# A gated mLSTM and convolution block: operand-group loads placed behind weight pieces, posts with a deadline, and another split of the down projection

## The chip, the cores and the metric

The kernel runs on one core of a Trainium2 chip, as one launch. The metric is the device time of one execution in microseconds (us). Before and after are compared by the median of several executions.

## The reference, cut to what matters

One residual block on x of 512 tokens by 2048 channels, all in float32. An RMS norm and one wide projection (w_in) give queries, keys, values, gates and convolution inputs; an mLSTM over 4 heads and a short causal convolution are each projected to 2048 channels (w_branch_m, w_branch_c), merged by sigmoid gates, projected by w_out and added to x. Then comes the channel mixer, which the down part of the change is about:

```python
hn = rmsnorm(h, norm_ffn_g)
u = causal_dwconv(hn @ w_up, ffn_conv_w, ffn_conv_b)      # 2048 -> 2 x 5504
gate, val = jnp.split(u, 2, axis=-1)
h = h + (jax.nn.silu(gate) * val) @ w_down                # 5504 -> 2048
return rmsnorm(h, norm_out_g)
```

## The kernel before, in words

**Products.** Every float32 operand is split into a high part, which ScalarE writes (a copy to the fp32r type), and a low part, which VectorE writes (the operand minus its high part). A product is three matmuls: high with high, high with low, low with high. Most of the work goes through a scheme with seven products in place of eight for a 2 x 2 block of tiles, so sums of weight tiles and of operand tiles have to be made first. Some pieces use all eight products and need no sums of weights; they are the last piece of each item in w_bc, w_bm, w_out and the down projection.

**Steps.** An item is a pair of output tiles. It takes `nq` steps; a step works off one weight piece (4 k tiles by 2 output tiles) against two operand groups, with 42 matmuls (48 with eight products). The first two and the last two items of a phase take turns, step by step. The phases, with the numbers of their steps: w_in 0 to 159, w_bc 160 to 175, w_bm 176 to 191, w_out 192 to 223, up 224 to 395, down 396 to 475, and 16 steps at the end (476 to 491) for the last three k tiles. The down projection is done in parts, given by `CHUNKS` (L37) as first k tile and number of pieces; each part adds its result to `h_d` in memory with an accumulating DMA from the POOL queue (L155).

**What a step issues** (loop from L291). In step s the low parts of piece s + 1 (L235, L189) and of the groups planned for s + 1 (L359) are written, the sums of piece s + 2 (L216, L221) and of the groups planned for s + 2 (L342, L347, L352, or L337 for groups used with eight products) are made, and the high parts follow. So a group planned for step k has its sums in step k - 2 and its low part in step k - 1, as piece k has. VectorE runs all this in the order written. When an item ends, ScalarE copies one product out of the accumulator (L303) and four VectorE additions (L309 to L312) in the next step form the result z.

**Loads.** A piece that needs sums is loaded in two stages: SP's queue fetches two tiles (L250, L251), and when they have landed, POOL's queue adds two others to them with accumulating DMAs (L253); a further DMA of SP brings the four tiles as they are (L260). A group takes two DMAs of 256 KB (L326). Pieces and groups share a ring of six raw buffers (`RAW`, L33). They are loaded in one fixed order, `order` (L1084): before, a group planned for step k stands just ahead of piece k. `load_next` (L1089) issues the next load when fewer than six loads are without their low parts; it counts finished low parts in `n_lo`. `loads` (L1097) is called at the end of each step and issues all it can; `load_to` forces the loads that the step needs. Groups of the up projection are scaled by ScalarE ahead of their sums: five are read from memory, the last three come straight from the item's z by two scalings (L394), with a raw buffer and no DMA.

**Posts.** What follows an item's end (normalizing, gates, convolution, silu, store) is a list of parts with costs, in us of VectorE. The planner adds 5.04 to a credit each step and takes off the cost of all VectorE work issued: 0.8 for the sums and 2.05 for the low parts of a piece (0 and 1.5 with eight products), 1.35 and 1.95 for a group (0.65 and 1.7; 1.35 more for sums that take in a z), 2.3 for the four additions. An up item's post has five parts: 1.2, 0, 1.4, 1.4 and 0.7. A part with a cost is issued only if credit is above half of it, unless the post is urgent. What is left when a later item ends is run at once, by `flush` (L1126), ahead of that item's copy (L303). For the up and down items that later item is three further on.

The loop that issues posts (L1385 to L1393), and the plan of the groups' steps (L1070 to L1081):

```python
cost, fn = x[1][0]
if not rush and cost and credit <= cost / 2:
    break
...
k = max(k, all_cells[n - 8].last + 3, t.after, t.spread)
if tasks[k]:
    k += 1
t.k = k
cells_at.setdefault(k, []).append(t)
tasks[k].append(t)
```

Of the kernel before, what the change touches and what calls it, by code (L numbers as in the profile page):

```python
# [33 lines left out]
NC = NW // 2  # L34
ACTS = 8
ALONE = ((0, 0), (1, 0), (0, 1), (0, 2))
CHUNKS = [(0, 4), (16, 3), (28, 3)]  # L37
K_LAST = 40


# [4 lines left out]
def kpair(c):  # L45

    q, r = divmod(c, 2)
    return 4 * q + r, 4 * q + 2 + r


class Item:


    def __init__(self, load, nq, xs, post, pre=None, eight=None):
        self.load, self.nq, self.xs, self.post, self.pre, self.eight = load, nq, xs, post, pre, eight
        self.p1_start, self.urgent, self.done = True, False, False
        self.set = self.num = self.z = self.buf = None
        self.p1_end = 2 * nq - (3 if eight == nq - 1 else 1)


class Task:


    def __init__(self, load, sums, hi, lo, ready=None):
        self.load, self.sums, self.hi, self.lo, self.ready = load, sums, hi, lo, ready
        self.wh = self.wl = None
        self.raw, self.cost, self.plain, self.after_end, self.pre = None, (0.8, 2.05), False, None, None


@with_exitstack  # L70
def tile_block(ctx: ExitStack, tc: tile.TileContext, xT, w1, w_v0, w_v1, w_v2, w_bm, w_bc, w_out, w_up, w_down,
# [13 lines left out]
    def nm(s):  # L85
        uid[0] += 1
        return f"{s}_{uid[0]}"

    def f(ap):
        return ap.bitcast(F32)  # L90
# [4 lines left out]
    def slots(t):  # L95
        return t.rearrange("p (s n) -> p s n", n=SW)

    def two(ap):
        return ap.unsqueeze(1).to_broadcast([P, 2, ap.shape[-1]])
# [215 lines left out]
    def cell_task(xs, c, d, scale=None, key=None, eight=False):  # L315

        k1, k2 = kpair(c) if isinstance(c, int) else c
        t = Task(None, None, None, None)

        def new_raw():  # L320
            t.raw = wp.tile([P, NW], F32, tag="raw", name=nm("xraw"), bufs=RAW)

        def load():
            new_raw()
            for dst, k in zip(t.two(), (k1, k2)):
                SP.dma_start(dst, d[k])  # L326

        def two_k():
            return (t.raw[:, :T], t.raw[:, T:2 * T]) if eight else (t.raw[:, 5 * SW:], t.raw[:, :2 * SW])

        def scaled():
            for ap, k in zip(two_k(), (k1, k2)):
                A.activation(ap, ap, AF.Copy, scale=scale(k))

        def diff():
            x = slots(t.raw)
            V.tensor_sub(x[:, 4:6], x[:, 0:4:2], x[:, 1:4:2])  # L337

        def t3():
            x = slots(t.raw)  # L340

            V.tensor_sub(x[:, 2:4], x[:, 1:6:4], two(x[:, 6]))  # L342

        def e():

            x = slots(t.raw)
            V.scalar_tensor_tensor(x[:, 4], x[:, 3], -1.0, x[:, 1], op0=ALU.mult, op1=ALU.subtract)  # L347

        def t4():

            x = slots(t.raw)
            V.scalar_tensor_tensor(x[:, 6], x[:, 4], -1.0, x[:, 0], op0=ALU.mult, op1=ALU.subtract)  # L352

        def hi():
            t.act = actp.tile([P, 2 * NW], F32R, tag="act", name=nm("act"))
            A.activation(t.act[:, :m], t.raw[:, :m], AF.Copy)  # L356

        def lo():
            V.tensor_sub(t.act[:, NW:NW + m], t.raw[:, :m], f(t.act[:, :m]))  # L359
            t.raw = None  # L360
            xs[t.cell] = t.act
            t.act = None

        t.load, t.sums, t.hi, t.lo, t.new_raw = load, [diff] if eight else [t3, e, t4], hi, lo, new_raw
        t.two, m = two_k, 6 * SW if eight else NW
        t.pre = scaled if scale else None
        t.cost = (0.65, 1.7) if eight else (1.35, 1.95)
        t.ready = (lambda: all(k in stored for k in key)) if key else None
        return t

    def direct_cell(xs, c, it, d=None, scale=None, key=None, eight=False):

        t = cell_task(xs, c, d, None, key, eight)
        cell_t3, cell_load = t.sums[0], t.load
        k1, k2 = kpair(c)

        def load():
            if d is not None:
                cell_load()
            else:  # L380
                t.new_raw()

        def t3():
            assert it.done
            a, b = t.two()
            V.tensor_add(a, a, it.z[:, :T])
            V.scalar_tensor_tensor(b, it.z[:, T:], -1.0, b, op0=ALU.mult, op1=ALU.subtract)
            it.z_read = True
            cell_t3()

        def scaled():
            assert it.done
            for ap, z, k in zip(t.two(), (it.z[:, :T], it.z[:, T:]), (k1, k2)):
                A.activation(ap, z, AF.Copy, scale=scale(k))  # L394
            it.z_read = True

        it.z_read = False
        t.load = load
        if d is not None:
            t.sums = [t3] + t.sums[1:]  # L400
        else:
            t.pre = scaled
        t.cost = (t.cost[0] + (1.35 if d is not None else 0), t.cost[1])
        t.after_end = it
        return t
# [464 lines left out]
    steps, items_all, all_cells = [], [], []  # L870
# [119 lines left out]

    for c, (k0, nq) in enumerate(CHUNKS):
        AA = {}
# [43 lines left out]
    def last_act():  # L1036
        t = Task(None, None, None, None)
        m = NL * T

        def load():  # L1040
            t.raw = wp.tile([P, NW], F32, tag="raw", name=nm("xraw"), bufs=RAW)
            for i in range(NL):
                SP.dma_start(t.raw[:, i * T:(i + 1) * T], a_d[K_LAST + i])

        def hi():
            t.act = actp.tile([P, 2 * NW], F32R, tag="act", name=nm("act"))
            A.activation(t.act[:, :m], t.raw[:, :m], AF.Copy)

        def lo():
            V.tensor_sub(t.act[:, m:2 * m], t.raw[:, :m], f(t.act[:, :m]))  # L1050
            t.raw = None
            plain["x"] = t.act
            t.act = None

        t.load, t.sums, t.hi, t.lo = load, [], hi, lo
        t.cost = (0, 1.7)
        t.ready = lambda: all(("a", K_LAST + i) in stored for i in range(NL))
        return t

    e_last = len(steps)  # L1060
    t = last_act()
    t.cell, t.first, t.last, t.after, t.spread, t.xs = "x", e_last, e_last + 15, 0, e_last - 4, plain
    all_cells.append(t)
    n_main = len(steps)
    steps.extend((l, 0) for l in lasts)


    tasks = [[] for _ in range(len(steps) + 1)]
    wt = [weight_task(it, q) if isinstance(it, Item) else last_weight(it.n) for it, q in steps]
    k, cells_at = 0, {}  # L1070
    for n, t in enumerate(all_cells):
        if n < 8:
            k = t.cell
        else:
            k = max(k, all_cells[n - 8].last + 3, t.after, t.spread)
            if tasks[k]:
                k += 1
            t.k = k
            cells_at.setdefault(k, []).append(t)
            assert k <= t.first, (n, k, t.first)  # L1080
        tasks[k].append(t)  # L1081
    for s, t in enumerate(wt):
        tasks[s].append(t)
    order = [t for ts in tasks for t in ts]  # L1084
    place = {id(t): i for i, t in enumerate(order)}
    at = [place[id(t)] for t in wt] + [len(order) - 1] * 8
    n_load, n_lo, held = [0], [0], [0]

    def load_next():  # L1089
        i = n_load[0]  # L1090
        if i == len(order) or i - n_lo[0] + held[0] == RAW or (order[i].ready and not order[i].ready()):
            return False
        order[i].load()
        n_load[0] += 1
        return True

    def loads():  # L1097
        while load_next():
            pass
# [5 lines left out]
    def lo_ops(t):  # L1105

        def done():
            n_lo[0] += 1

        if isinstance(t.wh, list):  # L1110
            return [lambda: t.lo(0), lambda: (t.lo(1), done())]
        return [lambda: (t.lo(), done())]
# [123 lines left out]
    for i in range(at[START]):  # L1236
# [4 lines left out]
        while todo_mm:  # L1241
            s, r = todo_mm[0]
            it, q = steps[s]
# [41 lines left out]
    credit = 0.0  # L1285
    urgent = {it.num for it in items_all if it.urgent}


    finals, lq, lsum = deque(), [], []

    for s in range(START, len(steps)):
        it, q = steps[s]
# [89 lines left out]
        if s >= START + hold:  # L1382
            credit = min(credit, 2.5)
            rush = not main or any(x[0] in urgent for x in posts)
            for x in list(posts)[:2]:  # L1385
                cost, fn = x[1][0]
                if not rush and cost and credit <= cost / 2:
                    break
                x[1].popleft()
                credit -= cost  # L1390
                fn()
                if not x[1]:
                    posts.remove(x)  # L1393
        for t in cells_at.get(s + 3, []):
            if t.pre and t.raw is not None and (not t.after_end or t.after_end.done):
                t.pre()
                t.pre = None
# [10 lines left out]
        if not main and it.n > 11 and finals:  # L1408
            for _ in range(2):
                if finals:  # L1410
                    last_scale(0, finals.popleft(), row0)
        loads()
    for l in lq:
        last_post(l)
    for l in lsum + lq:
# [68 lines left out]
```

## Time and profile before

| | us |
|---|---|
| median of 3 runs | 2645.81 (2645.74 to 2651.76) |
| the profiled execution, its own time | 2654.39 |
| its span, first to last instruction | 2652.7 |

The profile is of one execution of its own. Its span is 1.7 us shorter than that execution's time. TensorE is PE for matmuls and PEld for weight loads, VectorE is DVE, ScalarE is ACT, GpSimd is POOL, SyncE is SP. L and a number is a line of the kernel before. "<-" and a name stand for what ended an idle time.

### The profile page before, as it was taken

Reading aid. Unit: us, or ns where it says so; the run is one execution under the profiler, and the core shown is the slowest. Engines: PE = TensorE matmul, PEld = TensorE weight load, DVE = VectorE, ACT = ScalarE, POOL = GpSimd, SP = SyncE. Lnnn points to the kernel's source line nnn. Section 1 sums busy time; section 2 is a strip of 40 time slices with the busy share of each in tenths; the row PEclk is TensorE's granted clock in tenths of the full one; section 3 lists DMA queues with packets and bytes.
Section 4 is the critical chain, followed back from the end, with each engine's and each line's share of the span. In section 5 each row is a group of like instructions: output and inputs, shape, how many; then the busy total and the mean of one; then the engine's idle time right before and its main releaser. Section 6 shows DMA issues by size and latency. Waiting matters only on the chain.

```text
span 2652.7 us, 55503 instructions
## 1 busy us (share of the span) xinstructions
PE 2584.3 (97%) x21146; PEld 2564.9 (97%) x21146; DVE 2112.7 (80%) x3308; ACT 1291.1 (49%) x1748; POOL 796.4 (30%) x922
## 2 busy tenths in 40 slices
PE   8999999999999999899999999999999989999998
PEld 8999999999999999899899999999999989999997
DVE  8577778886777888877989888888888887676756
ACT  6444554546556543345555445444444544444433
POOL 2443333333333111221333333333333223232320
PEclk8999999999999999999999999999999999999999
DMA  7798989998898797887998889989888888898976
GB/s 216 181 228 229 240 223 253 221 252 225 231 248 219 227 298 208 218 244 209 236 224 227 221 221 227 225 219 225 222 222 220 209 219 210 200 239 195 233 173 203
DMA packets 462557, 592.55 MB, mean 223 GB/s; under 512 B 42784, under 2 KB 296736, under 8 KB 462288
## 3 DMA queue, kind: packets, MB, share of 16 engines
q1 hardware_dynamic: 301968, 419.79, 50.4%
q0 software_dynamic: 133088, 124.04, 31.4%
q10 hardware_dynamic: 27232, 45.17, 4.7%
q8 instruction: 165, 2.70, 0.4%
q14 instruction: 104, 0.85, 0.1%
HBM read 531.17 MB, written 57.67 MB: 222 GB/s over the span
## 4 chain that ended last, share of the span: by engine, by line
PE 54%; DVE 6%; DMA 3%; issue 2%; ACT 0%; POOL 0%; DVEq 0%; SPq 0%; POOLq 0%; ACTq 0%
PE bank L281 18%; PE bank L279 18%; PE bank L280 17%; DMA raw<-in_w_down_dram 2%; DVE wl L235 1%; DVE act L359 1%; DMA raw<-in_w_out_dram 1%; DVE z L310 0%; PE bank L440 0%; PE bank L1164 0%; PE bank L1165 0%; PE bank L1166 0%; DMA raw<-in_w_up_dram 0%; DVE z L309 0%; DMA h_d<-z 0%
## 5 line engine op out<-in xcount | busy, mean ns | idle before, releaser
L281 PE MATMUL bank<-act,wl 128*128 128x256 f32 x6760 | 1922.7, 284 | 33.5 <-DVE wl L235 28.5
L279 PE MATMUL bank<-act,wh 128*128 128x256 f32 x6760 | 1931.1, 286 | 14.3 <-ACT z L303 5.8
L280 PE MATMUL bank<-act,wh 128*128 128x256 f32 x6760 | 1919.3, 284 | 0.0
L281 PEld LDWEIGHTS bank<-act,wl 128*128 128x128 f32 x6760 | 1303.9, 193 | 39.4 <-DVE wl L235 33.4
L279 PEld LDWEIGHTS bank<-act,wh 128*128 128x128 f32 x6760 | 1304.2, 193 | 18.8 <-ACT z L303 6.5
L231 ACT ACTIVATE wh<-raw 128x896 fp32r<-128x896 f32 x856 | 812.1, 952 | 1036.9 <-PE bank L280 679.5
L280 PEld LDWEIGHTS bank<-act,wh 128*128 128x128 f32 x6760 | 1304.3, 193 | 2.8 <-issue 1.7
L235 DVE TENSOR_TENSOR wl<-raw,wh 128x896 fp32r<-128x896 f32 x856 | 929.1, 1087 | 343.1 <-PE bank L281 231.7
L253 POOL DMA_DIRECT2D raw<-in_w_up_dram x344 | 298.5, 941 | 603.4 <-DMA raw<-in_w_up_dram 371.9
L253 POOL DMA_DIRECT2D raw<-in_w_dram x280 | 244.1, 961 | 527.1 <-DMA raw<-in_w_dram 344.9
L216 DVE TENSOR_TENSOR raw<-raw 128x256 f32<-128x256 f32 x428 | 179.6, 420 | 37.3 <-DMA raw<-in_w_down_dram 23.1
L253 POOL DMA_DIRECT2D raw<-in_w_down_dram x112 | 100.9, 1032 | 282.2 <-DMA raw<-in_w_down_dram 107.4
L221 DVE TENSOR_TENSOR raw<-raw 128x256 f32<-128x256 f32 x428 | 179.0, 418 | 0.3
L309 DVE TENSOR_TENSOR z<-bank,z 128x512 f32<-128x512 f32 x131 | 89.8, 686 | 38.4 <-ACT z L303 28.3
L356 ACT ACTIVATE act<-xraw 128x1792 fp32r<-128x1792 f32 (+1 forms) x52 | 85.6, 1646 | 60.2 <-DVE xraw L352 49.5
L184 ACT ACTIVATE wh<-raw 128x256 fp32r<-128x256 f32 x96 | 40.0, 416 | 131.0 <-PE bank L280 118.6
L359 DVE TENSOR_TENSOR act<-xraw,act 128x1792 fp32r<-128x1792 f32 (+1 forms) x52 | 101.7, 1955 | 0.0
L686 DVE TENSOR_TENSOR z<-z,rstd 128x1024 f32<-128x1024 f32 x83 | 100.8, 1217 | 0.2 <-ACT rstd L457 0.2
L189 DVE TENSOR_TENSOR wl<-raw,wh 128x256 fp32r<-128x256 f32 x96 | 40.5, 421 | 64.3 <-PE bank L281 37.3
L310 DVE TENSOR_TENSOR z<-bank,z 128x512 f32<-128x512 f32 x131 | 89.6, 684 | 1.7
L312 DVE TENSOR_TENSOR z<-bank,z 128x512 f32<-128x512 f32 x131 | 89.5, 683 | 0.0
L253 POOL DMA_DIRECT2D raw<-in_w_out_dram x48 | 41.8, 983 | 131.5 <-DMA raw<-in_w_out_dram 91.0
(214 smaller groups left out, 1380.3 us busy)
## 6 DMA issues: line engine op xcount, KB each, us to landing
raw<-in_w_up_dram SPq DMA_DIRECT2D x172, 512.0 KB, 5.7
raw<-in_w_dram SPq DMA_DIRECT2D x144, 512.0 KB, 5.9
raw<-in_w_up_dram SPq DMA_DIRECT2D x344, 128.0 KB, 3.9
raw<-in_w_up_dram POOLq DMA_DIRECT2D x344, 128.0 KB, 5.4
raw<-in_w_down_dram SPq DMA_DIRECT2D x80, 512.0 KB, 5.1
raw<-in_w_dram SPq DMA_DIRECT2D x280, 128.0 KB, 4.3
raw<-in_w_dram POOLq DMA_DIRECT2D x280, 128.0 KB, 5.4
raw<-in_w_out_dram SPq DMA_DIRECT2D x32, 512.0 KB, 5.2
```

The costliest lines, as they stand in the source:

```text
L216: V.tensor_add(x[:, 6], x[:, 5], x[:, 0])
L221: V.tensor_add(x[:, 2], x[:, 6], x[:, 1])
L231: A.activation(seven(t.wh[r]), half(r), AF.Copy)
L235: V.tensor_sub(seven(t.wl[r]), half(r), seven(f(t.wh[r])))
L253: G.dma_start(at(i), a21, accum_op=ALU.add)
L279: PE.matmul(ps, h, xh, start=start, stop=False, skip_group_check=True)
L280: PE.matmul(ps, h, xl, start=False, stop=False, skip_group_check=True)
L281: PE.matmul(ps, l, xh, start=False, stop=stop, skip_group_check=True)
L309: return [lambda: V.tensor_add(z[:, 0:4:3], b0, two(z[:, 1])), lambda: V.tensor_add(z[:, 1:3], b1, two(z[:, 3])), lambda: V.tensor_add(z[: ...
L310: lambda: V.tensor_add(z[:, 1:3], b1, two(z[:, 3])),
L359: V.tensor_sub(t.act[:, NW:NW + m], t.raw[:, :m], f(t.act[:, :m]))
L686: V.tensor_mul(sb_pair(it.z), sb_pair(it.z), two(rstd))
```

## The change

It does three things. A group planned for step k is now loaded ahead of piece k + 2 instead of piece k (k + 1 if ScalarE scales it from memory, k + 3 if it is scaled from a z); since low parts are then no longer finished in the order of the loads, each load has a mark `done`, and `n_lo` counts the marked ones from the front. A part of a post is issued without credit when as many parts are left as there are steps to the step in which `flush` would run them. The down projection's parts are 12, 12 and 16 k tiles (3, 3 and 4 pieces an item) instead of 16, 12 and 12. Besides, `loads()` stands ahead of the scaling of the groups of step s + 3 and of the last stores, not behind them.

```diff
-CHUNKS = [(0, 4), (16, 3), (28, 3)]
+CHUNKS = [(0, 3), (12, 3), (24, 4)]
...
+        self.done, self.behind = False, 2
...
-        t.pre = scaled if scale else None
+        if scale:
+            t.pre, t.behind = scaled, 1
...
-            t.pre = scaled
+            t.pre, t.behind = scaled, 3
...
-    k, cells_at = 0, {}
+    low, cells_at = 0, {}
     for n, t in enumerate(all_cells):
         if n < 8:
             k = t.cell
         else:
-            k = max(k, all_cells[n - 8].last + 3, t.after, t.spread)
-            if tasks[k]:
+            k = max(low, all_cells[n - 8].last + 3, t.after, t.spread)
+            if k in cells_at:
                 k += 1
-            t.k = k
+            t.k = low = k
             cells_at.setdefault(k, []).append(t)
             assert k <= t.first, (n, k, t.first)
+            k = min(k + t.behind, len(steps))
         tasks[k].append(t)
...
         i = n_load[0]
+        while n_lo[0] < i and order[n_lo[0]].done:
+            n_lo[0] += 1
...
         def done():
-            n_lo[0] += 1
+            t.done = True
...
+    ends = {it.num: s for s, (it, q) in enumerate(steps[:n_main]) if q == it.nq - 1}
+
+    def due(num):
+
+        n = num + 2
+        return ends.get(n if n < len(items_all) and (n < 42 or items_all[n].pre) else n + 1, len(steps))
...
-                if not rush and cost and credit <= cost / 2:
+                if not rush and cost and credit <= cost / 2 and len(x[1]) < due(x[0]) - s:
                     break
...
+        loads()
         for t in cells_at.get(s + 3, []):
             if t.pre and t.raw is not None and (not t.after_end or t.after_end.done):
                 t.pre()
...
-        loads()
```

## Rows read from the trace of the kernel before

**Rows 1.** The page, busy time of the engines: us, share, instructions

```profile
PE 2584.3 (97%) x21146; PEld 2564.9 (97%) x21146; DVE 2112.7 (80%) x3308; ACT 1291.1 (49%) x1748; POOL 796.4 (30%) x922
```

**Rows 2.** Windows: length, busy us (instructions) per engine, granted clock, DMA share, GB/s

```profile
2120.00:2215.00 95.00, 82.69 (x654) 81.27 (x653) 79.72 (x115) 44.19 (x56) 24.67 (x29) 0.96 0.81 213
1245.00:1305.00 60.00, 52.98 (x406) 51.73 (x405) 53.73 (x82) 37.31 (x45) 15.96 (x19) 0.94 0.82 214
1080.00:1120.00 40.00, 33.19 (x253) 32.28 (x252) 36.00 (x47) 16.51 (x19) 8.68 (x10) 0.91 0.72 193
895.00:920.00 25.00, 22.49 (x186) 22.09 (x185) 20.88 (x31) 10.39 (x17) 3.50 (x4) 1.00 0.64 190
2320.00:2345.00 25.00, 23.44 (x195) 23.20 (x194) 23.27 (x33) 13.14 (x16) 5.92 (x7) 1.00 0.77 207
2440.00:2475.00 35.00, 32.03 (x250) 31.39 (x249) 27.34 (x43) 17.26 (x21) 7.04 (x8) 0.95 0.75 201
1400.00:1600.00 200.00, 200.00 (x1669) 200.00 (x1668) 179.13 (x264) 98.82 (x121) 68.73 (x80) 1.00 0.90 225
```

**Rows 3.** Waits of TensorE over the span: us in total, times, longest

```profile
PE bank L281 <- DVE wl L235: 28.5, 21, 2.5
PE bank L279 <- ACT z L303: 5.8, 3, 4.7
```

**Rows 4.** Line groups, VectorE L216, rows 2's first six stretches: busy, mean ns, idle before

```profile
L216 DVE TENSOR_TENSOR raw<-raw 128x256 f32<-128x256 f32 x13 | 5.5, 421 | 8.1 <-DMA raw<-in_w_down_dram 7.0 <-DMA raw<-in_w_up_dram 1.1
...
L216 DVE TENSOR_TENSOR raw<-raw 128x256 f32<-128x256 f32 x8 | 3.3, 417 | 3.8 <-DMA raw<-in_w_up_dram 3.8
...
L216 DVE TENSOR_TENSOR raw<-raw 128x256 f32<-128x256 f32 x5 | 2.1, 423 | 3.7 <-DMA raw<-in_w_out_dram 3.7
...
L216 DVE TENSOR_TENSOR raw<-raw 128x256 f32<-128x256 f32 x3 | 1.3, 419 | 3.6 <-DMA raw<-in_w_bc_dram 3.6
...
L216 DVE TENSOR_TENSOR raw<-raw 128x256 f32<-128x256 f32 x3 | 1.3, 422 | 1.6 <-DMA raw<-in_w_down_dram 1.6
...
L216 DVE TENSOR_TENSOR raw<-raw 128x256 f32<-128x256 f32 x4 | 1.7, 421 | 5.8 <-DMA raw<-in_w_down_dram 5.8
```

**Rows 5.** Timeline of TensorE, four waits: start, us, instruction [idle before, releaser]

```profile
2140.64 0.58 PE L281 MATMUL bank<-act,wl 128*128 128x256 f32 x1 [2.47 <-DVE wl L235]
...
2155.50 0.38 PE L281 MATMUL bank<-act,wl 128*128 128x256 f32 x1 [1.57 <-DVE wl L235]
...
2202.11 0.58 PE L279 MATMUL bank<-act,wh 128*128 128x256 f32 x1 [4.67 <-ACT z L303]
...
2459.93 0.39 PE L281 MATMUL bank<-act,wl 128*128 128x256 f32 x1 [1.89 <-DVE wl L235]
```

**Rows 6.** Windows of 3.4 us behind three of these waits, columns as in rows 2

```profile
2140.43:2143.85 3.42, 3.21 (x15) 3.21 (x16) 3.42 (x5) 2.06 (x3) 0.00 (x0) 0.50 0.57 119
2155.49:2158.90 3.41, 3.40 (x28) 3.40 (x29) 3.01 (x5) 0.30 (x1) 1.75 (x2) 1.00 0.95 222
...
2201.87:2205.29 3.42, 3.18 (x15) 3.18 (x16) 3.17 (x6) 1.98 (x3) 0.02 (x1) 0.50 0.71 152
```

**Rows 7.** Timelines of SP, POOL and DVE: a piece, and a group's two DMAs

```profile
2438.59 0.33 SPq L250 DMA_DIRECT2D raw<-in_w_down_dram  x1
...
2444.19 1.79 POOL L253 DMA_DIRECT2D raw<-in_w_down_dram  x2 [9.85 <-DVE xraw L342]
...
2451.11 0.43 DVE L216 TENSOR_TENSOR raw<-raw 128x256 f32<-128x256 f32 x1 [4.51 <-DMA raw<-in_w_down_dram]
...
2445.83 0.81 SPq L326 DMA_DIRECT2D xraw<-a_d  x2
```

**Rows 8.** All groups' loads (L326) over the span

```profile
DMA to landing us min/median/max: 2.4/4.5/7.5
```

**Rows 9.** Timeline of ScalarE, the last group of the up projection

```profile
1293.40 1.32 ACT L394 ACTIVATE xraw<-z,pcol 128x512 f32<-128x512 f32 x2
```

## The prediction

> **What bounds the kernel now.** First the busy time by engine: TensorE is busy 97% of the span [rows 1], so anything to be won lies in a few places. The stretches say where. In the steady part of the up projection 200 us hold 1669 matmuls at full clock, 0.1198 us each [rows 2]. Multiply the matmuls of each other stretch by that and take it from the stretch's length: up to down loses 95.0 - 654 x 0.1198 = 16.6 us; into the up projection 60.0 - 406 x 0.1198 = 11.4; into w_out 40.0 - 253 x 0.1198 = 9.7; into w_bc 25.0 - 186 x 0.1198 = 2.7; from the first down part to the second 25.0 - 195 x 0.1198 = 1.6; from the second to the third 35.0 - 250 x 0.1198 = 5.0. Together 47 us, all where a new set of operand groups is made ready.
>
> The waits of TensorE say for whom: mostly the low part of a weight piece from VectorE (L235), then the copy of the first product by ScalarE (L303) [rows 3]. And VectorE itself, in these same stretches, stood before a piece's first sum (L216) until the piece's DMA landed: 8.1, 3.8, 3.7, 3.6, 1.6 and 5.8 us, 26.6 in all [rows 4]. So two things are mixed there: VectorE has more to do than the 5.04 us of a step, and it also waits for pieces.
>
> A TensorE wait has a second price. Behind waits of 2.47 and 4.67 us the granted clock was 0.50 (1.2 GHz) for 3.4 us, behind one of 1.57 it stayed 1.00 (2.4 GHz) [rows 5, 6]. A half clock of 3.4 us costs 1.7.
>
> **The change, part by part.** I number steps as the document does.
>
> *Order of loads.* Six raw buffers go round, so a load can be issued only when the low part of the load six places before it is written. Before, group k stands just ahead of piece k. Take the first down piece, 396: ahead of it stand group 396, piece 395, group 395, piece 394, group 394, piece 393; piece 393's low part is written in step 392, the load goes out then, and the sums want it in step 394, two steps. After, with groups two places later, the six ahead are group 394, 395, 394, group 392, 393, 392: issued in step 391, three steps. The same count gives pieces 395 to 399 two steps before, and 4, 3, 3, 2 and 3 after; the other two down transitions are alike, with a lead of 2 left at the third step of each part. Into w_out pieces 194 and 195 go from 2 to 4 and 3, into w_bc 161 and into up 224 from 2 to 3. What a step is worth: a piece's first half went out at 2438.59, its accumulating DMA at 2444.19, and the sums began at 2451.11, 12.5 us later [rows 7]. Two steps of 5 us are too few, three are enough. So the waits of rows 4 should fall to about 1 us at each down part.
>
> The price is on the groups. Their lead falls from 3 steps to 1 in eighteen places (4 of the 6 groups in each of two down parts, 6 of 8 in the third, 4 more into w_bc and w_out), and one group of the up projection gets its buffer only in the step of its own sums. A group's two DMAs take 0.8 us to issue [rows 7] and 2.4 to 7.5 to land, median 4.5 [rows 8]: some 5.3, with ends of 3.2 and 8.3. Between the low part that frees its buffer and its own first subtraction VectorE does, by the planner's costs, 1.35 + 2.85 = 4.2 us for the fifth or sixth group of a part, a step's 5.0 for the third, 6 to 7 for others. So late by about 1.5 and 0.7 us at each part, 2.2 in sum (a group could also be on time, 0, or 8.3 - 4.2 = 4.1 late); 1.2 into w_out, 0.4 into w_bc. Into the up projection the last group has no DMA, but ScalarE's two scalings of 1.32 us [rows 9] now stand in front of its subtraction: 1.3.
>
> A rule speaks against this part. In the rows the DMA engines are busy 0.81, 0.82 and 0.72 in the three worst stretches, and 0.90 in the steady part where nothing waits [rows 2]: there is room, and the pieces are late because they start late. The Trainium skill, DMA: Bandwidth & Descriptors, section Issuing engines are not separate DMA queues, says that DMAs of all queues run on the same 16 engines and interleave. By that a moved load only changes places with another one, which is the first rival; by the rows the sum below stands.
>
> *Posts by a deadline.* Before, parts of a post wait for credit, which is negative in a transition, and what is left is run in a lump ahead of the copy L303. By the credit rule 4.7 us of item up 41 fall on step 403, and TensorE then waited 4.67 us for that copy, with 3.4 us of half clock behind [rows 5, 6]: 4.7 + 1.7 = 6.4 us. After, the deadline puts out one part a step from 398 on, and 2.1 us of the lump are left, at step 401. In steps 398 to 402 VectorE is then asked for 6.4 + 2.2 + 4.9 + 7.2 + 5.8 = 26.5 us against 25.2: 1.3 given back. In the w_out phase the lump of 2.7 at step 203 goes too; that stretch is not among those that lose most, so I take 0.6, with 0 and 2.7 as ends. Moving the issue of loads ahead of the scaling and the last store: these are other queues (SP and POOL against ScalarE), 0; were SP to wait there it would hold nothing but later loads.
>
> *Parts of 12, 12 and 16 k tiles.* Steps, matmuls, stores and pieces with eight products are as many as before. Two groups leave the first transition for the third. In the first they came in steps 399 to 401, where VectorE was asked for less than a step: 0 there. In the third, steps 443 to 446 now ask for 7.1 + 6.5 + 6.2 + 4.8 = 24.6 against 20.2, 4.4 too much. A lead of VectorE covers most of it: in up to down, 7.0 us of work planned beyond the steps' time and 8.1 of waits cost TensorE 16.6 - 6.4 - 1.7 = 8.5, so 6.6 were hidden. I charge 0.5.
>
> **The sum**, in us saved. Up to down: 6.4 - 1.3 for posts; VectorE's waits 8.1 - 3.2 (2.2 for groups, 1 for a piece) = 4.9, of which I let three quarters, 3.7, reach TensorE, because of that lead; one half clock of 1.7: 10.5. Into up: 3.8 - 1.3 = 2.5, in full, for VectorE is busy without a break behind that wait, and half of one 1.7: 3.4. Into w_out: 3.7 - 1.2 + 0.6 = 3.1. Into w_bc: 3.6 - 0.4, held to 2.4 of the 2.7 lost. First to second part: 1.6 - 2.2 = -0.6. Second to third: 5.8 - 3.2 = 2.6, half of a 1.7 behind the 1.89 us wait [rows 5], less 0.5: 3.0. Sum 21.8. The profiled execution is 2654.39 us (span 2652.7), so 2632.6 there; against the median of the runs, 2645.81, which is 8.6 lower, 2624.0.
>
> **The rivals.** *The waits only change their names.* If the moved loads delay each other, the 26.6 us of rows 4 come back on the groups, and only the posts win: 6.4 - 1.3 + 0.6 = 5.7, 2640.1. For it: the groups' lead of one step, and 0.90 of DMA busy as a ceiling not far off. Against it: 0.72 to 0.82 in the stretches themselves [rows 2], and that a group needs one transfer where a piece needs two in a row. Chance 0.13.
>
> *Late groups make it slower.* VectorE runs in order: where it stands before a late group, the low parts of the next piece stand behind it, and TensorE behind those. I have charged 3 x 2.2 + 1.2 + 0.4 + 1.3 = 9.5 us for groups; without them the gain is 31.3. Over nineteen groups the point of decision is 31.3 / 19 = 1.6 us late each. At 2.5 us (a landing of 5.9 behind 0.8 of issue against 4.2) they cost 47.5: 16.2 slower, 2662. For it: a landing of 7.5 was seen. Against it: the median of 4.5, and six of them have 6 us or more of other work ahead. Chance 0.07.
>
> *More than I forecast.* The pieces and groups all come in time and no wait reaches the length that is followed by half clock. Four fifths of 26.6 are 21.3, the posts 6.4, four half clocks 6.8: 34.5, 2611. For it: the half clock hangs on small differences (1.57 against 1.89 [rows 5]). Against it: planned work of VectorE beyond 5.04 us a step stays, by the planner's costs some 13 us into the up projection alone. Chance 0.15. That the change does nothing is excluded by the order worked out above.
>
> **How the numbers follow.** The forecast, 2624, has 0.65. Its own bounds: groups with a DMA on time, 8.2 less (2616), or the worst one of each part 4.1 late instead of 1.5 (2632). Low is the third case, 2611; high takes in the first rival, 2641. What a measurement of this kernel can tell from no change is about 0.3%, 7.9 us: 2637.9 to 2653.7. Faster: 0.65 + 0.15 and the better edge of the first rival, 0.83; the same 0.11; slower 0.06.
>
> **What the profile after would show.** Right: VectorE's waits at L216 for DMA below 10 us in the six stretches, some new ones at L342 or L337 for the groups' DMAs of 1 to 2 us; no TensorE wait on L303 over 1 us near the end of the first down pair; half clocks gone near 2140 and 2202; the steady up stretch unchanged at 0.1198 us a matmul. Wrong: waits for the groups that sum to over 25 us, pieces that are late with three steps of lead, or a TensorE wait ahead of step 401 for the two parts that are still run in a lump.

## Result: faster by 0.67%, inside the range, with one stretch worse than before

Over six runs each the median is 2631.64 us (2628.04 to 2635.23) after and 2648.27 us (2645.74 to 2655.48) before: ratio 0.9933, interval 0.9916 to 0.995, so 13 to 22 us faster, against 21.8 forecast. The profiled execution went from 2654.39 to 2634.42 us, its span from 2652.7 to 2632.7: 20.0.

To see where, I take each stretch from the first matmul of its first step to the first of the step behind it, less 0.1198 us for each matmul of the products. Into the up projection after, for example, is steps 220 to 235, 1233.91 to 1330.97 us, 684 matmuls: 97.06 - 81.94 = 15.1 us lost. (Matmuls of norms and posts are in this loss in all kernels alike, so only differences count.)

| stretch (steps before) | lost before | lost after | won | forecast |
|---|---|---|---|---|
| into w_bc (158 to 163) | 3.1 | 0.1 | 3.0 | 2.4 |
| into w_out (190 to 211) | 11.0 | 7.3 | 3.7 | 3.1 |
| into up (220 to 235) | 13.5 | 15.1 | -1.6 | 3.4 |
| up to down (390 to 411) | 18.0 | 4.4 | 13.6 | 10.5 |
| first to second part (420 to 435; after 412 to 427) | 2.1 | 2.0 | 0.1 | -0.6 |
| second to third (444 to 463; after 436 to 455) | 6.2 | 3.2 | 3.0 | 3.0 |
| behind the last of the steps 0 to 475 | 63.5 | 65.5 | -2.0 | none |

The six stretches give 21.8, to the digit the forecast, but that is luck: one term was 5.0 too high and four others together as much too low, one of them by 3.1. The end of the kernel takes 2.0 back, and 0.2 lie elsewhere.

The windows of after, for the same places and in the same order as [rows 2], and with the same columns:

```profile
894.80:919.80 25.00, 25.00 (x211) 25.00 (x209) 23.95 (x39) 13.00 (x21) 3.50 (x4) 1.00 0.77 221
1076.70:1116.70 40.00, 35.89 (x277) 35.19 (x276) 36.71 (x50) 17.59 (x22) 9.30 (x12) 0.91 0.73 203
1237.90:1297.90 60.00, 50.22 (x393) 48.65 (x392) 52.32 (x78) 36.27 (x43) 16.54 (x19) 0.97 0.81 215
2114.60:2209.60 95.00, 91.50 (x759) 90.89 (x758) 82.37 (x123) 47.84 (x68) 24.65 (x27) 1.00 0.85 217
2260.00:2285.00 25.00, 23.43 (x195) 23.23 (x195) 24.90 (x37) 14.65 (x16) 4.66 (x6) 1.00 0.79 212
2380.70:2415.70 35.00, 33.55 (x278) 33.15 (x277) 32.35 (x52) 19.25 (x23) 9.37 (x11) 1.00 0.95 253
1400.00:1600.00 200.00, 200.00 (x1669) 200.00 (x1668) 179.06 (x264) 98.78 (x121) 69.43 (x80) 1.00 0.91 224
```

Up to down fits 759 matmuls into the 95 us where 654 stood before, at full clock throughout; into up has 393 where there were 406. The steady part is the same to the matmul.

VectorE's waits and TensorE's over the span (us in total, times, longest); L217 is L216 of before, L343 is L342, L236 is L235 and L304 is L303, and against [rows 3]:

```profile
DVE raw L217 <- DMA raw<-in_w_down_dram: 7.8, 5, 2.9
DVE raw L217 <- DMA raw<-in_w_up_dram: 2.9, 1, 2.9
DVE raw L217 <- DMA raw<-in_w_bc_dram: 0.3, 1, 0.3
...
DVE xraw L343 <- DMA xraw<-a_d: 1.6, 2, 1.0
DVE xraw L343 <- ACT xraw L396: 1.3, 1, 1.3
DVE xraw L343 <- ACT xraw L334: 1.0, 1, 1.0
...
PE bank L282 <- DVE wl L236: 19.7, 13, 2.5
PE bank L280 <- ACT z L304: 1.5, 2, 0.8
```

The sums of pieces in the two stretches with the largest error, grouped as in [rows 4], up to down first and into up second:

```profile
L217 DVE TENSOR_TENSOR raw<-raw 128x256 f32<-128x256 f32 x12 | 5.0, 420 | 0.5 <-DMA raw<-in_w_down_dram 0.5
...
L217 DVE TENSOR_TENSOR raw<-raw 128x256 f32<-128x256 f32 x7 | 2.9, 420 | 2.9 <-DMA raw<-in_w_up_dram 2.9
```

In the window into w_bc this wait is 0.3 and in the other three 0.0, so in these windows 26.6 us of [rows 4] have become 3.7. But the windows end early. Over the whole stretches of the table above, VectorE's waits before a piece's first sum fell from 36.6 to 11.0 us: 7.4 of the 11.0 fall on the first two pieces of the third item in the second and third down part, which waited 8.5 us before. One row for each of these two places, before and then after:

```profile
2350.71 0.43 DVE L216 TENSOR_TENSOR raw<-raw 128x256 f32<-128x256 f32 x1 [2.50 <-DMA raw<-in_w_down_dram]
2488.07 0.42 DVE L216 TENSOR_TENSOR raw<-raw 128x256 f32<-128x256 f32 x1 [2.40 <-DMA raw<-in_w_down_dram]
```

```profile
2291.81 0.43 DVE L217 TENSOR_TENSOR raw<-raw 128x256 f32<-128x256 f32 x1 [2.94 <-DMA raw<-in_w_down_dram]
2435.59 0.42 DVE L217 TENSOR_TENSOR raw<-raw 128x256 f32<-128x256 f32 x1 [2.54 <-DMA raw<-in_w_down_dram]
```

They cost TensorE little: after loses 1.1 us at the later of the two places and nothing at the other.

Of the groups with a DMA only two came late, by 1.6 us in all. The 4.67 us wait of TensorE for the copy is 0.67 (at 2175.37), and no stretch of half clock is left between 1263 and 2604 us, where before had four besides the one at 1266.6.

### The profile page after: what moved, and what is told of

Read it like the earlier page. It is cut to its first block, busy times and chain, and to the rows that moved or that the text cites. A ratio compares the mean times of both kernels' runs of the same rounds, so it can differ in the third digit from the quotient of the medians.

```text
span 2632.7 us, 55496 instructions
## 1 busy us (share of the span) xinstructions
PE 2577.4 (98%) x21146; PEld 2559.9 (97%) x21146; DVE 2112.0 (80%) x3308; ACT 1291.6 (49%) x1748; POOL 797.9 (30%) x922
## 4 chain that ended last, share of the span: by engine, by line
PE 67%; DVE 5%; DMA 2%; issue 1%; ACT 0%; SPq 0%; POOL 0%; DVEq 0%; ACTq 0%; POOLq 0%
PE bank L282 22%; PE bank L280 22%; PE bank L281 22%; DVE act L360 1%; DVE wl L236 1%; PE bank L1170 0%; PE bank L442 0%; PE bank L1171 0%; PE bank L1172 0%; DMA h_d<-z 0%; DVE xraw L343 0%; DMA raw<-in_w_down_dram 0%; PE bank L639 0%; DVE z L311 0%; DMA xraw<-h_d 0%
## 5 line engine op out<-in xcount | busy, mean ns | idle before, releaser
L282 PE MATMUL bank<-act,wl 128*128 128x256 f32 x6760 | 1919.0, 284 | 23.1 <-DVE wl L236 19.7
L282 PEld LDWEIGHTS bank<-act,wl 128*128 128x128 f32 x6760 | 1301.5, 193 | 27.1 <-DVE wl L236 23.1
L236 DVE TENSOR_TENSOR wl<-raw,wh 128x896 fp32r<-128x896 f32 x856 | 930.3, 1088 | 343.0 <-PE bank L282 233.7
L217 DVE TENSOR_TENSOR raw<-raw 128x256 f32<-128x256 f32 x428 | 179.8, 420 | 11.4 <-DMA raw<-in_w_down_dram 7.8
```

The lines of the kernel that those rows point to most:

```text
L217: V.tensor_add(x[:, 6], x[:, 5], x[:, 0])
L236: V.tensor_sub(seven(t.wl[r]), half(r), seven(f(t.wh[r])))
L282: PE.matmul(ps, l, xh, start=False, stop=stop, skip_group_check=True)
```

## Experiments

All kernels compute the whole output. The table has each kernel's median, its ratio to before with the interval, and the losses of its profile in the stretches above. Each experiment's ratio is to the kernel before as run beside it: 2649.14 (e1 to e4), 2648.05 (e5 to e8) and 2647.95 us (e9 to e11).

| kernel | us | ratio | w_bc | w_out | up | up to down | 1st to 2nd | 2nd to 3rd |
|---|---|---|---|---|---|---|---|---|
| after | 2631.64 | 0.9933 (0.9916 to 0.995) | 0.1 | 7.3 | 15.1 | 4.4 | 2.0 | 3.2 |
| e1 order alone | 2636.88 | 0.9952 (0.9938 to 0.9967) | 0.1 | 8.2 | 14.9 | 11.9 | 1.2 | 2.0 |
| e2 posts alone | 2641.03 | 0.997 (0.9957 to 0.9984) | 3.9 | 10.2 | 12.2 | 9.8 | 3.5 | 5.8 |
| e3 parts alone | 2653.18 | 1.0013 (1.0002 to 1.0024) | 3.9 | 9.5 | 12.7 | 15.0 | 6.1 | 8.6 |
| e4 z groups two behind | 2630.11 | 0.9926 (0.9913 to 0.994) | 0.1 | 7.3 | 16.0 | 4.5 | 1.4 | 2.2 |
| e5 order and posts | 2626.98 | 0.9926 (0.9913 to 0.9939) | 0.1 | 7.2 | 15.1 | 5.2 | 1.0 | 1.9 |
| e6 three behind | 2644.13 | 0.9983 (0.9974 to 0.9992) | 0.1 | 7.2 | 14.9 | 8.1 | 5.4 | 13.6 |
| e7 up groups earlier | 2622.55 | 0.9908 (0.9893 to 0.9923) | 0.1 | 7.2 | 11.1 | 5.2 | 1.3 | 1.3 |
| e8 loads last | 2629.94 | 0.9932 (0.992 to 0.9944) | 0.1 | 7.2 | 18.1 | 4.5 | 1.5 | 2.0 |
| e9 one behind | 2641.35 | 0.9962 (0.9944 to 0.998) | 2.0 | 8.9 | 14.6 | 5.0 | 2.7 | 7.5 |
| e10 as e7, z three behind | 2623.01 | 0.9906 (0.9888 to 0.9923) | 0.1 | 7.2 | 12.2 | 5.2 | 1.0 | 1.9 |
| e11 before, up groups earlier | 2646.71 | 0.9994 (0.9985 to 1.0003) | 3.6 | 9.0 | 12.1 | 16.5 | 1.6 | 6.1 |

**The three edits one by one.** e1 is after without the deadline and with the old parts:

```diff
-CHUNKS = [(0, 3), (12, 3), (24, 4)]
+CHUNKS = [(0, 4), (16, 3), (28, 3)]
...
-                if not rush and cost and credit <= cost / 2 and len(x[1]) < due(x[0]) - s:
+                if not rush and cost and credit <= cost / 2:
```

> Only the order of loads of the change, with 16, 12 and 12 k tiles and posts by credit alone. My theory (pieces' lead is worth most): TensorE's loss falls into w_bc by 3, into w_out by 3 to 4, in up to down by 4 to 6 and at the last down transition by 3, nothing into up; the 4.7 us wait on L303 near step 404 stays, with half clock behind it. 10 to 14 us faster than before. Rival (waits only change names): VectorE's waits for groups take the place of those for pieces, 0 to 3 us faster. Rival (posts do the work): under 6 us faster.

e2 is before with `ends`, `due` and this condition:

```diff
-                if not rush and cost and credit <= cost / 2:
+                if not rush and cost and credit <= cost / 2 and len(x[1]) < due(x[0]) - s:
```

> Only the deadline of the posts, loads in the order of before, 16, 12 and 12 k tiles. My theory: the wait on L303 of 4.7 us and its half clock go, the 26.6 us of VectorE's waits for pieces stay: 5 to 7 us faster. Rival (the lump only filled time that the late pieces cost anyway): 0 to 2 us faster. Rival (posts do the work): 10 us or more.

e3 is before with the new parts alone:

```diff
-CHUNKS = [(0, 4), (16, 3), (28, 3)]
+CHUNKS = [(0, 3), (12, 3), (24, 4)]
```

> Only the parts of 12, 12 and 16 k tiles. My theory: two groups move between transitions and the lump ahead of L303 shrinks from 4.7 to 3.5 us of VectorE work at the end of the first pair; 0 to 3 us faster, VectorE's waits for pieces about as before. Rival (the first transition is what costs, and the split is what lightens it): 5 us or more faster. Rival: the third transition, with eight groups, loses what the first wins: no difference.

The order alone wins 0.48% (12.7 us), the posts alone 0.30% (7.9), and the parts alone cost 0.13% (3.4). Together 17.2, against 17.7 (0.67%) for the whole: within what such runs tell, they add up. First e1, TensorE's timeline and its waits, then e2, VectorE's waits:

```profile
2190.29 0.58 PE L280 MATMUL bank<-act,wh 128*128 128x256 f32 x1 [4.46 <-ACT z L304]
...
PE bank L280 <- ACT z L304: 5.2, 2, 4.5
```

```profile
DVE raw L216 <- DMA raw<-in_w_down_dram: 22.6, 11, 4.6
...
DVE raw L216 <- DMA raw<-in_w_bc_dram: 5.0, 2, 4.5
```

Each edit takes away one kind of wait and leaves the other. With the order alone the wait for the copy stays, with 6.8 us of half clock behind it, and up to down still loses 11.9; with the posts alone the pieces are as late as before (22.6 us here, 23.1 over the span of before), and it loses 9.8. With both it loses 5.2 (e5).

The parts alone make the transitions between parts worse, 6.1 and 8.6 us instead of 2.1 and 6.2. In the first to second stretch VectorE waits 10.5 us for pieces, where before waited 6.1. The last two rows are a third item's first two pieces, which waited 4.2 in before too; what is new is the part's first piece, with 4.77:

```profile
2275.22 0.43 DVE L216 TENSOR_TENSOR raw<-raw 128x256 f32<-128x256 f32 x1 [4.77 <-DMA raw<-in_w_down_dram]
...
2294.22 0.43 DVE L216 TENSOR_TENSOR raw<-raw 128x256 f32<-128x256 f32 x1 [1.18 <-DMA raw<-in_w_down_dram]
...
2308.20 0.42 DVE L216 TENSOR_TENSOR raw<-raw 128x256 f32<-128x256 f32 x1 [3.82 <-DMA raw<-in_w_down_dram]
...
2311.05 0.42 DVE L216 TENSOR_TENSOR raw<-raw 128x256 f32<-128x256 f32 x1 [0.75 <-DMA raw<-in_w_down_dram]
```

Why a lead of two steps falls shorter there than in the old place was not settled.

**Do the parts earn their place beside the other two?** e5 is after with the old parts (the first hunk of e1 alone).

> The changed kernel with the parts left at 16, 12 and 12 k tiles. Theory A (the three parts of the change add up, and the split alone cost 3 to 4 us): 18 to 22 us faster than before, 2 to 4 faster than the changed kernel, won between the down parts. Theory B (the split pays once the loads are in order, because two groups leave the first transition): slower than the changed kernel by 1 to 4 us, lost in up to down; that stretch then loses 2 us or more beyond the 4.7 of the changed kernel.

Not that these runs can tell: 0.9926 without them, 0.9933 with them, intervals overlapping. By the profiles e5 wins 1.0 and 1.3 in the later transitions and gives 0.8 back in up to down.

**The stretch that got worse.** In after, the timelines of SP, POOL and VectorE show one piece into the up projection, and VectorE's two waits for ScalarE's scalings:

```profile
1242.53 0.33 SPq L251 DMA_DIRECT2D raw<-in_w_up_dram  x1
...
1245.96 1.75 POOL L254 DMA_DIRECT2D raw<-in_w_up_dram  x2 [4.90 <-DVE xraw L348]
...
1255.42 0.43 DVE L217 TENSOR_TENSOR raw<-raw 128x256 f32<-128x256 f32 x1 [2.92 <-DMA raw<-in_w_up_dram]
...
1249.08 0.69 DVE L343 TENSOR_TENSOR xraw<-xraw 128x512 f32<-128x512 f32 x1 [1.04 <-ACT xraw L334]
1290.17 0.69 DVE L343 TENSOR_TENSOR xraw<-xraw 128x512 f32<-128x512 f32 x1 [1.29 <-ACT xraw L396]
```

TensorE's timeline behind them:

```profile
1258.89 0.38 PE L282 MATMUL bank<-act,wl 128*128 128x256 f32 x1 [1.89 <-DVE wl L236]
...
1294.98 0.39 PE L282 MATMUL bank<-act,wl 128*128 128x256 f32 x1 [2.11 <-DVE wl L236]
```

Piece 224, for which VectorE waited 3.84 us before, came in time. Piece 225, whose lead is two steps before and after, went out at 1242.53 and was wanted 10 us later; it was there after 12.9, the time that [rows 7] gave (12.5). Before, the wait for 224 had put that moment off by itself. e4 takes away the wait at 1290:

```diff
-            t.pre, t.behind = scaled, 3
+            t.pre, t.behind = scaled, 2
```

> The changed kernel, but groups scaled from a z stand two pieces later, not three. Then the last group of the up projection has its buffer a step earlier and its scalings come at the end of step 226. My theory: VectorE's wait of 1.29 us for the scaling (L396) and TensorE's wait of 2.11 us in step 229 go: 1 to 2.5 us faster than the changed kernel, seen in that stretch of the profile; pieces 227 to 230 still in time. Rival: pieces come later by the slot and the wait comes back at L217: no gain, or 1 to 2 us slower.

The wait is gone, but 225 was 4.7 us late in that execution, with 10.2 us of half clock in the stretch where after had 3.4, and the time is not told apart from after's (0.9926 against 0.9933, overlapping). So e7 plans three of the eight groups of the up projection one step earlier, with e4's edit and the old parts; e10 is e7 without e4's edit; e11 is before with the spread alone:

```diff
-               cell_task(HH, c, h_d, g_ffn, [("h", c)]) for c in range(8)], (-4, -2, -1, 0, 2, 3, 4, 5))
+               cell_task(HH, c, h_d, g_ffn, [("h", c)]) for c in range(8)], (-4, -3, -2, -1, 2, 3, 4, 5))
```

> Order and posts of the change, parts of 16, 12 and 12 k tiles, groups scaled from a z two pieces later, and the up projection's second to fourth groups planned one step earlier each. Theory (into up is bound by VectorE's work being planned too close together, and by piece 225's lead of two): the stretch into up loses 15 us in the changed kernel, here 9 to 12; with the split left out 21 to 26 us faster than before. Rival (only the pieces' lead counts there, and 224 now has 2): the stretch still loses 14 to 16, as fast as order and posts alone.

> As the run with the up projection's groups planned earlier, but the groups scaled from a z stand three pieces later, as in the change. If the earlier plan is what lowered the loss into up from 15.3 to 11.3 us: 11 to 13 here, with the 1.3 us wait for L396 back. If the place of the z groups did it: 14 or more, as with order and posts alone.

> The kernel before, with only the up projection's second to fourth groups planned one step earlier each. If VectorE's work was planned too close together, this wins without the new order of loads: 2 to 4 us faster than before, the stretch into up down from 13.7 to 10 to 12. If the pieces' lead is what binds there: no gain, since the groups' loads then stand ahead of pieces 221 to 223 and make these late: within 1 us, or slower.

VectorE's waits in e7, and its window into up, for the same place as the third above:

```profile
DVE xraw L343 <- ACT xraw L334: 2.8, 2, 1.7
DVE raw L217 <- DMA raw<-in_w_up_dram: 1.4, 2, 1.2
```

```profile
1232.60:1292.60 60.00, 54.00 (x426) 52.66 (x426) 55.34 (x87) 38.48 (x49) 17.71 (x21) 0.97 0.84 232
```

426 matmuls in the 60 us instead of 393, and a loss of 11.1 instead of 15.1, with the same 3.4 us of half clock in the stretch as after. By the count of the six buffers the earlier plan also gives piece 225 three steps of lead instead of two; its wait falls from 2.92 to 1.23. What of the 4.0 us is that lead, and what the VectorE work moved ahead, was not separated. e7 is the best of all: its runs, 2620.88 to 2626.02, lie wholly below those of after, though the ratios' intervals touch (0.9893 to 0.9923 against 0.9916 to 0.995). e10 keeps the 1.3 us wait at L396 and loses 1.1 us more into up, but its time is the same as e7's, so the earlier plan seems to count and not e4's edit. Against e5, which has neither, the medians are 4 us apart and the intervals still overlap. In the kernel before the earlier plan is worth nothing that can be told (0.9994): its profile loses 12.1 into up in place of 13.5, and 1.4 us is too little for these runs.

**How far behind?** e6 puts a group that is read from memory without scaling three places later instead of two, e9 one:

```diff
-        self.done, self.behind = False, 2
+        self.done, self.behind = False, 3
```

> The changed kernel, but groups read from memory without scaling stand three pieces later instead of two: their loads go out in the very step of their sums (lead 0) at four of six or more groups of each down part. If late groups are dear as in the second rival of the prediction (VectorE stands before a group and everything queues behind it): each late by 3 to 5 us, VectorE waits of 30 us or more at L343 and L338 for DMAs, 10 to 25 us slower than the changed kernel. If DMAs of a group land far sooner than charged, or the lead of VectorE hides it: under 5 us slower.

> The changed kernel, but groups read from memory without scaling stand one piece later instead of two: the pieces of a down transition get leads of mostly 3 with one 2, the groups 2 to 4. If what counts is that no piece is left with a lead of two steps, a small part of the waits comes back: 1 to 5 us slower than the changed kernel, in the down stretches, with VectorE waits at L217 of 3 to 10 us. If the second place matters little: the same within 1 us, and groups' waits at L343 gone.

VectorE's waits in e6, then its timelines of VectorE and TensorE at the worst place:

```profile
DVE xraw L343 <- DMA xraw<-a_d: 16.7, 9, 3.2
...
DVE xraw L338 <- DMA xraw<-a_d: 4.8, 2, 4.7
...
DVE xraw L343 <- DMA xraw<-yc_d: 1.5, 1, 1.5
```

```profile
2451.54 0.43 DVE L217 TENSOR_TENSOR raw<-raw 128x256 f32<-128x256 f32 x1 [3.46 <-DMA raw<-in_w_down_dram]
...
2455.13 0.38 PE L280 MATMUL bank<-act,wh 128*128 128x256 f32 x1 [3.41 <-ACT z L304]
```

With no step of lead the groups are late by 23.0 us in all, the copy waits behind them, and the loss from second to third part is 13.6. That is 0.50% (13.2 us) worse than after. With one place (e9) pieces at the transitions are late again, in VectorE's waits:

```profile
DVE raw L217 <- DMA raw<-in_w_down_dram: 9.1, 8, 2.2
...
DVE raw L217 <- DMA raw<-in_w_bc_dram: 2.9, 2, 2.2
```

After's row for w_down has 7.8 us, but nearly all of it at the third items named above; there e9 waits 5.3, and 3.8 elsewhere in the down parts, where after waits 0.5. In w_bc, w_out and the last transition e9 loses 1.9, 1.6 and 4.3 more: 0.29% (7.7 us) worse, with intervals that overlap a little (0.9944 to 0.998 against 0.9916 to 0.995). By the medians two places is the best of the three.

**The place of the issue.** e8 is after with `loads()` back at the end of the step.

```diff
-        loads()
         for t in cells_at.get(s + 3, []):
...
                     last_scale(0, finals.popleft(), row0)
+        loads()
```

> The changed kernel with loads() at the end of the step, as before the change. Prediction's step: the move is worth 0, within 1 us of the changed kernel. Rival: the groups scaled by ScalarE get their buffers only after the scaling's turn, so their scaling slips into the step of their sums: into up loses 2 to 5 us more, with VectorE waiting for L334 or L396.

The time is the same, 0.9932. Into up its profile loses 3.0 more, with 3.9 us of waits for L396 in place of 1.3 and three stretches of half clock in place of one, so the place may not be quite without effect there; the median doesn't show it.

## Why the prediction came out right, and which steps were wrong

**Bound and mechanism: right.** The signs that it named are there: 3.7 us of VectorE's waits for pieces in the windows of [rows 2] (below 10), 1.6 us of new waits for groups, 0.67 us for the copy, the half clocks near 2140 and 2202 gone, and the steady stretch unchanged. By e1 and e2 the gain is the sum of the two causes that were kept apart: posts 7.9 where the working gave 5.7, the order 12.7 where it gave 16.6 (21.8 less 5.7, and without the 0.5 charged for the parts).

**Three steps of lead are not enough everywhere.** The pieces at the third items have three or four steps of lead by the prediction's own count, before and after, and were late in both, by 8.5 and 7.4 us. That is one of its signs of being wrong, and the kernel before already had it, outside the windows that the prediction read. It put the rest of each down part at about 1 us; over the stretches it is 0.5, 3.5 and 3.9. It hardly touched the time, because TensorE lost 1.1 us there. At this place steps are no good measure of time: piece 426 was wanted 8.6 us after its load went out (2280.24), not three steps of 5.

**Into up, the step that failed: 3.4 forecast, 1.6 lost.** The working took the lead of the one piece that had waited, 224, and let its 3.8 us reach TensorE in full. It didn't count the next piece's lead, which the change leaves at two steps. By the working's own 12.5 us for a piece, two steps of 5 are too few, so 225 was to be late as soon as 224 was not. TensorE's loss step by step fits: steps 223 to 225 lose 6.3 us, 6.1 before, so nothing was won there. The 1.3 us for the scaling at L396 was right to the digit (1.29), and TensorE's 2.11 us wait follows it: step 229 loses 2.4 instead of 1.0, most of the 1.6. The scaling at L334 added 1.04 of VectorE's time that was not in the sum. Of the stretch's two half clocks one went (step 227), but that won only 0.2: the step loses 4.8 us with it and 4.6 without, for the wait of 2.25 us ahead of it stayed. e7 shows a profile with 4.0 us less lost in this stretch.

**Groups' DMAs, mis-sized: 8.2 charged, 1.6 measured.** That was 1.5 us for the fifth or sixth group of a part, in the working with ends of 0 and 4.1; 0 was nearly right. That e6's groups, with no step of lead, were late by 23.0 us, and e9's pieces by 3.8 us in the rest of the down parts, where after's are by 0.5, shows how near two places lies to both edges. The rival of late groups is thus a true mechanism of this kernel with its point one place further on.

**Up to down, mis-sized: 10.5 forecast, 13.6 won.** Of the 3.2 us left over for late groups and one late piece, 0.5 came (the piece in the grouped row above), and three quarters of the 2.7 between are 2.0. By steps, 395 to 400 lose 3.4 us instead of 10.6: 7.2 won where the sum had 5.4 for the order. The step of the copy (404) loses nothing instead of 6.3, step 408 nothing instead of 1.0 (that goes with the deadline: e2 and e5 have it so, e1 not), and step 402, with the 0.67 us wait, loses 0.9: 6.3 won where the sum had 5.1 for the posts. Both half clocks went, as counted: the fourth window has 1.00 throughout.

**First to second and second to third part.** 0.1 and 3.0 against -0.6 and 3.0. These hide two errors that cancel: the order wins more there than I gave it (e1: 0.9 and 4.2) and the new parts take some back. I charged 0.5 for the parts; alone they cost 3.4 us (0.5 to 6.4).

**End of the kernel, not in the sum.** TensorE's wait of 1.48 us in the last phase is the same in both kernels, but in after half clock follows it. After's timeline and window, then before's:

```profile
2602.49 0.70 PE L1416 MATMUL bank<-mC,ones 128*128 128x256 f32 x2 [1.48 <-DVE mC L453]
...
2604.00:2607.50 3.50, 3.50 (x18) 3.50 (x19) 2.36 (x5) 1.71 (x3) 0.00 (x0) 0.51 0.43 150
```

```profile
2624.55 0.70 PE L1403 MATMUL bank<-mC,ones 128*128 128x256 f32 x2 [1.48 <-DVE mC L451]
...
2626.00:2629.40 3.40, 3.40 (x31) 3.40 (x31) 3.40 (x8) 2.07 (x4) 0.00 (x0) 1.00 0.46 154
```

18 matmuls against 31 in about 3.4 us: some 1.5 us of the 2.0 lost there. It isn't the change's doing as such, for the same wait is followed by full clock in e1, e2, e3, e4, e5, e7, e9 and e10, which hold parts of it.

**Rivals.** "The waits only change their names" gave 2640.1. It is refuted: over the six stretches of the table VectorE waits 12.6 us for groups and pieces' sums together, where before waited 36.6 for pieces alone, and the order alone wins 12.7 us (e1). The Trainium skill, DMA: Bandwidth & Descriptors, section Issuing engines are not separate DMA queues, lets DMAs of all queues share 16 engines. At a DMA share of 0.73 to 0.95 in the windows above, the loads moved ahead did not cost the others what they won, so here the start of a load decided more than the room. "Late groups make it slower" needed 1.6 us for each of nineteen groups; it was 1.6 us in all. "More than I forecast" (2611) needed every piece in time and no wait long enough to be followed by half clock; 225 and the end of the kernel speak against it, and even e7, at 0.9908, wins 24 us and not 34.5.

## What to carry to other kernels

When a shared ring of buffers is reordered, count the lead of every transfer in the transition against its measured time from issue to use, also of those that never waited: the first late one was covering the next. Read the waits over the whole stretch, not in a window that ends with the first of them. Move the transfers with one stage behind those with two, place by place, and measure one place to either side; here both neighbours cost 8 to 13 us by the medians. Of a change with several parts run each alone: one of these three paid nothing.

## What the runs showed of the hardware that was not expected

**The start of the kernel differs from one execution to the next.** TensorE's first stretch of half clock is 17.1 us long in the profile of before, 13.7 in after's and 6.8 in e5's; windows of before, then of e5:

```profile
10.50:27.60 17.10, 13.29 (x61) 12.99 (x61) 16.75 (x23) 13.83 (x17) 1.98 (x2) 0.50 0.77 236
```

```profile
11.20:18.00 6.80, 3.86 (x16) 3.56 (x17) 6.66 (x10) 6.54 (x9) 0.00 (x0) 0.50 0.85 248
18.00:27.60 9.60, 9.60 (x84) 9.60 (x83) 9.39 (x13) 7.08 (x8) 1.98 (x2) 1.00 0.76 222
```

Steps 0 to 7 lose 21.9 us in before, 21.4 in after and 17.5 in e5, and the code there is the same in all of them. So 4.4 of the 29.8 us by which e5's span is shorter than before's are not e5's, and spans of single profiles are to be compared stretch by stretch. It may be part of why runs of the kernel before spread over 13 us (2642.52 to 2655.59 in 18 runs); a run without a profile can't show that.

**The same wait has two sequels.** A 1.48 us wait at the same place was followed by half clock in after, e6, e8 and e11, and by full clock in the other kernels, and the 1.57 us wait of [rows 5] by full clock too. The 2.25 us wait in step 227 is the same in before and after, with the clock behind it half in one and full in the other; before first:

```profile
1287.00 0.52 PE L281 MATMUL bank<-act,wl 128*128 128x256 f32 x1 [2.25 <-DVE wl L235]
...
1287.10:1290.50 3.40, 3.40 (x16) 3.40 (x17) 3.40 (x4) 2.83 (x4) 0.00 (x0) 0.50 0.60 109
```

```profile
1280.17 0.38 PE L282 MATMUL bank<-act,wl 128*128 128x256 f32 x1 [2.25 <-DVE wl L236]
...
1280.20:1283.60 3.40, 3.40 (x28) 3.40 (x29) 3.40 (x4) 2.90 (x4) 0.00 (x0) 1.00 0.53 111
```

So the length of a wait alone, by which the prediction told its half clocks apart, does not decide. What does, no run here shows.
